# Hybrid decoder block on one core: adaLN row sums by products with a column of ones, part of them inside the second norm, the gate in the last columns' weights, last rows in halves, another order

## The chip, the cores and the metric

The kernel runs on one core of a Trainium2 chip. The metric is device time in microseconds (us) of one execution; lower is better. A kernel's time is the median of its runs. The profile is one further execution; its span runs from the first to the last instruction.

PE is the matmul engine and PEld its weight load, DVE the vector engine, ACT the scalar engine, POOL the general engine, SP the one whose queue issues most DMAs.

## The reference

One decoder block over 256 tokens of width 2048, in f32. A vector `c` gives, through one large product, six rows: shift, scale and gate for the two halves of the block.

```python
mod = silu(c) @ w_ada + b_ada                    # 2048 x 12288
sh1, sc1, g1, sh2, sc2, g2 = split(mod, 6)
h = rms_norm(x, norm1_g) * (1 + sc1) + sh1
q, k, v, gb, gc, xt = split(h @ w_in, 6)         # 2048 x 6144
attn = causal_attention(rms_norm(q), rms_norm(k), v)   # 8 heads of 128
conv = gb * causal_dwconv(gc * xt, conv_w, conv_b)
x = x + g1 * (concat(rms_norm(attn), rms_norm(conv)) @ w_out)
h2 = rms_norm(x, norm2_g) * (1 + sc2) + sh2
u_gate, u_up = split(causal_dwconv(h2 @ w_ffn_up), 2)  # 2048 x 11264
x = x + g2 * ((silu(u_gate) * u_up) @ w_ffn_down)      # 5632 x 2048
```

With 256 tokens the attention has a single block, so it is plain causal attention.

## The kernel before

Weights stream from HBM once, in 512 KB pieces (`raw`, 128 x 1024). Every weight and activation is split into a high part and a low part, `hi` on ACT (L938) and `lo = raw - hi` on DVE or POOL (L949), and each matmul of f32 precision is made of three in a faster format: high by high, high by low, low by high (L1185 to L1187). In the up projection the two products with the high weights are one matmul of 512 columns (L1536), and the third has 256 (L1540).

The work is a list of **slots**: the input projection (its twelve column groups of 512, named q0 to x1, in the order of `CFG['turns']`), the output projection (A and C parts), then the up projection z and the down projection D in four segments. A slot is up to four weight blocks and their matmuls. Function `slot(i)` writes out, in this order: the split of the weights of slot i + 2 (`split_hi`, `split_lo`), the small tasks that fall due, and the matmuls of slot i. `CFG['hi_late']` lists the slots whose split comes after the early tasks instead of ahead of them. The engines run what is written in that order; `CFG['move']`, `after`, `mid`, `pre`, `carry` shift tasks by slots or positions, and how many accumulation steps stand between them. Nothing else decides the order: an instruction waits only for its operands and buffers.

**adaLN** (class `Ada`). Parts 0 to 5 are the six rows of 2048 values; SH1 = 0, SC1 = 1, G1 = 2, SH2 = 3, SC2 = 4, G2 = 5. Each part is made in column groups. Some accumulate on PE (`crep` as weights, L1025, four row groups of the array at once, tiles `ada`), the others on DVE, a step for every 128 rows of the matrix (L1042). Either way the result is 128 x n, and the row of values is the sum over its 128 partitions. For shift and scale it is needed as a column, 128 channels on 128 partitions: `cols` transposes every chunk of 128 columns by PE (L1080, bank `adac`), DVE sums along the free axis (L1082, `adaz`), and `finish` writes A (scale) or B (shift). `evac` brings the accumulators of PE to SBUF (`adae`). For the gates, `spread` and `broadcast` make rows `gB` of 128 equal partitions.

**The start** is a hand-written order, `CFG['start']`: `sc` and `sh` are the scale and shift products of the first two chunks (their halves 0 and 1, then `e` for evacuation and `c` for the columns), `tr` and `out` transpose x and copy it out (`xn`, `xnT`), `p n b` splits block b of slot n, `h` makes the modulated input, `go n h` issues matmuls of slot n. It also sets the order in which the first loads are issued on SP's queue.

**The second norm** (`norm2`, L1397 on): squares on ACT, a root by DVE and ACT, a diagonal `n2d` by DVE, a product `n2b` on PE that spreads it, then `h2_chunks` for the first eight chunks of the up projection's input. PE has one load of adaLN ahead of `n2b` and a part of it behind.

**The end.** Columns are worked in pairs of groups of 512, f = 0, 1 and then 2, 3, both token halves t in each. `gate_down` folds the gate and the residual into x1 for the first segments. In the last segment `evac_down` multiplies the bank by the gate row (L1504), adds x1 (L1505) and stores 128 x 512 (L1506); the last slots belong to f = 2 and f = 3.

**Sums and seeds.** A column group whose partial sum leaves PSUM is added by DVE when it comes back (L1207), or, where `CFG['seed']` names it, copied back into PSUM by ACT first (L1194) and copied out by ACT again (L1205).

## Time and profile before

| | us |
|---|---|
| median of 3 runs | 1174.42 (1174.08 to 1176.89) |
| the profiled execution | 1174.33 |
| its span | 1172.2 |
| DMA moved | 320.21 MB, mean 273 GB/s |
| 42 to 100 us: PE busy of 58.0 | 58.0 |
| 165 to 427 us: PE busy of 262.0 | 262.0 |
| 435 to 1139 us: PE busy of 704.0 | 704.0 |

A row of the profile's groups names the line, the engine, the operation, what it writes and reads, the shape and the count, then busy time, mean duration in ns, idle time of the engine before it and what ended that. In the timeline a row has its start and length. PE's matmuls overlap, and their ends are modelled: how long one takes in a stream is read from the distance of starts, not from a row's length. An f32 product shows as two records, a transpose and a matmul of the split format as one.

### The profile page before, as it was taken

How to read it: one execution, taken by the hardware profiler on the slowest of the kernel's cores; microseconds unless marked ns; L12 is line 12 of the kernel's file. 1: busy time of each engine (PE TensorE's matmuls, PEld its weight loads, DVE VectorE, ACT ScalarE, POOL GpSimd, SP SyncE). 2: the span in 40 equal slices, each digit the busy share in tenths (PEclk: the TensorE clock that was granted, in tenths of full speed). 3: DMA queues.
4: the chain of work that ended last, by engine and by line, in shares of the span. 5: the costliest groups of instructions: out<-in, count | busy, mean ns of one | idle time of the engine just before them, and what ended most of it. 6: DMA issues, size and time to landing. Idle time of an engine off the chain costs nothing.

```text
span 1172.2 us, 17007 instructions
## 1 busy us (share of the span) xinstructions
PE 1148.8 (98%) x5945; PEld 960.4 (82%) x5945; DVE 928.4 (79%) x1318; ACT 635.9 (54%) x981; POOL 169.4 (14%) x103
## 2 busy tenths in 40 slices
PE   4999999999999999999999999999999999999998
PEld 2778788888777878888888888888888888888886
DVE  4669989997888989999999544768887897666785
ACT  4664455469665445546676445555435554445461
POOL 0668684530001111000000000000000000000000
PEclk9999999999999999999999999999999999999999
DMA  9999999995799989986565755576887877875541
GB/s 350 404 406 364 387 381 373 397 389 171 228 395 319 344 292 358 377 276 208 159 208 186 235 179 179 174 234 216 284 296 272 301 243 229 284 256 175 171 153 72
DMA packets 205381, 320.21 MB, mean 273 GB/s; under 512 B 13816, under 2 KB 112300, under 8 KB 205296
## 3 DMA queue, kind: packets, MB, share of 16 engines
q1 hardware_dynamic: 202336, 314.68, 77.2%
q10 hardware_dynamic: 2352, 4.22, 1.3%
q8 instruction: 46, 0.75, 0.3%
q14 instruction: 39, 0.32, 0.1%
q0 software_dynamic: 608, 0.23, 0.1%
HBM read 314.87 MB, written 4.21 MB: 272 GB/s over the span
## 4 chain that ended last, share of the span: by engine, by line
PE 91%; DVE 5%; DMA 2%; ACT 1%; issue 1%; SPq 0%; ACTq 0%; DVEq 0%
PE z L1536 27%; PE z L1540 14%; DVE ada L1042 2%; PE ada L1025 1%; PE mv L1185 1%; PE mv L1187 1%; PE mc L1185 1%; PE mv L1186 1%; PE mc L1187 1%; PE mc L1186 1%; PE mx L1185 1%; PE mx L1187 1%; PE mx L1186 1%; PE mg L1185 1%; PE mg L1187 1%; PE mg L1186 1%
## 5 line engine op out<-in xcount | busy, mean ns | idle before, releaser
L938 ACT ACTIVATE hi<-raw 128x1024 fp32r<-128x1024 f32 (+1 forms) x401 | 401.1, 1030 | 324.7 <-PE z L1536 100.9
L949 DVE TENSOR_TENSOR lo<-raw,hi 128x1024 fp32r<-128x1024 f32 x342 | 399.0, 1204 | 99.8 <-ACT hi L938 94.3
L1536 PE MATMUL z<-h,hi 128*128 128x512 f32 x1408 | 328.6, 390 | 0.0
L1536 PEld LDWEIGHTS z<-h,hi 128*128 128x128 f32 x1408 | 261.4, 188 | 52.7 <-DVE h L1431 0.3
L1042 DVE SCALAR_TENSOR_TENSOR ada<-raw,csil,ada 128x512 f32<-128x512 f32 (+2 forms) x215 | 188.9, 891 | 3.6
L949 POOL TENSOR_TENSOR lo<-raw,hi 128x1024 fp32r<-128x1024 f32 x59 | 147.0, 2511 | 274.3 <-ACT hi L938 231.6
L1540 PEld LDWEIGHTS z<-h,lo 128*128 128x128 f32 x1408 | 174.8, 192 | 3.4
L1540 PE MATMUL z<-h,lo 128*128 128x256 f32 x1408 | 176.0, 283 | 0.0
L1101 POOL MEMSET gb<- 128x512 f32 x2 | 1.0, 524 | 491.9 <-DVE uy L1475 491.9
L1452 DVE TENSOR_TENSOR ub<-z,ub 128x256 f32<-128x256 f32 x120 | 43.7, 416 | 34.9 <-ACT ub L1449 34.7
L1449 ACT ACTIVATE ub<-z 128x256 f32<-128x256 f32 x120 | 39.4, 382 | 30.9 <-PE z L1536 30.8
L1468 ACT ACTIVATE uy<-ub,vcols 128x256 f32<-128x256 f32 x88 | 45.6, 594 | 6.8 <-DMA gr<-gs 6.7
L1473 DVE SCALAR_TENSOR_TENSOR uy<-ub,vcols,uy 128x255 f32<-128x255 f32 x88 | 42.1, 478 | 5.7 <-ACT uy L1468 5.6
L1475 DVE SCALAR_TENSOR_TENSOR uy<-ub,vcols,uy 128x254 f32<-128x254 f32 x88 | 42.5, 483 | 3.1
L1484 ACT ACTIVATE gh<-uy 128x512 fp32r<-128x512 f32 x22 | 13.8, 629 | 38.8 <-DVE uy L1482 38.8
L1478 ACT ACTIVATE uy<-uy 128x512 f32<-128x512 f32 x22 | 13.9, 633 | 37.9 <-DVE uy L1475 37.9
L1185 PE MATMUL mq<-hi,h 128*128 128x512 f32 x64 | 25.8, 403 | 3.8 <-DVE xnT L2026 2.8
L1485 DVE TENSOR_TENSOR gl<-uy,gh 128x512 fp32r<-128x512 f32 x22 | 15.2, 692 | 18.0 <-ACT gh L1484 18.0
L1025 PE MATMUL ada<-raw,crep 128*32 128x512 f32 (+1 forms) x224 | 26.2, 565 | 2.6 <-DVE rst L882 1.9
L1185 PE MATMUL mc<-hi,h 128*128 128x512 f32 x64 | 25.5, 398 | 0.5 <-ACT pa_q L1205 0.5
L1185 PE MATMUL mg<-hi,h 128*128 128x512 f32 x64 | 25.7, 402 | 0.0
L1185 PE MATMUL mv<-hi,h 128*128 128x512 f32 x64 | 25.3, 395 | 0.2 <-DVE pa_g L1207 0.2
(570 smaller groups left out, 1913.7 us busy)
## 6 DMA issues: line engine op xcount, KB each, us to landing
raw<-in_w_ada_dram SPq DMA_DIRECT2D x180, 512.0 KB, 6.5
raw<-in_w_ffn_up_dram SPq DMA_DIRECT2D x352, 256.0 KB, 4.5
raw<-in_w_in_dram SPq DMA_DIRECT2D x95, 512.0 KB, 7.3
raw<-in_w_ffn_down_dram SPq DMA_DIRECT2D x76, 512.0 KB, 4.3
raw<-in_w_out_dram SPq DMA_DIRECT2D x32, 512.0 KB, 5.4
raw<-in_w_ada_dram SPq DMA_DIRECT2D x24, 256.0 KB, 6.3
raw<-in_w_ffn_down_dram SPq DMA_DIRECT2D x24, 256.0 KB, 3.8
xr<-in_x_dram SPq DMA_DIRECT2D x4, 512.0 KB, 6.0
```

The costliest lines, as they stand in the source:

```text
L938: act(piece(his, "hi")[:, :m], t[:, :m], AF.Copy)
L949: (nc.gpsimd if pool in (i + 1, 3) else V).tensor_tensor(out=piece(los, "lo")[:, :m], in0=t[:, :m], in1=hi[:, :m].bitcast(F32), op=ALU.sub ...
L1042: V.scalar_tensor_tensor(out=self.acc[n], in0=v, scalar=csil[:, i:i + 1], in1=acc, op0=ALU.mult, op1=ALU.add)
L1185: mm(o, a, hi[k], start=(first and k == 0 and not seeded), stop=False, skip_group_check=True)
L1186: mm(o, a, lo[k], start=False, stop=False, skip_group_check=True)
L1187: mm(o, b, hi[k], start=False, stop=(last and k == nk - 1), skip_group_check=True)
L1452: V.tensor_tensor(out=d, in0=zp[grp][ft][:, :256], in1=d, op=ALU.add)
L1468: act(y, b, AF.Identity, bias=fcols[3][:, i:i + 1], scale=fcols[2][:, i:i + 1])
L1473: V.scalar_tensor_tensor(out=y[:, 1:], in0=b[:, :255], scalar=fcols[1][:, i:i + 1], in1=y[:, 1:], op0=ALU.mult, op1=ALU.add)
L1475: V.scalar_tensor_tensor(out=y[:, 2:], in0=b[:, :254], scalar=fcols[0][:, i:i + 1], in1=y[:, 2:], op0=ALU.mult, op1=ALU.add)
L1536: mm(zp[grp][ft], blk(hi, j)[:, ft * P:(ft + 1) * P], h2T[k + j], start=k + j == ks[0], stop=k + j == ks[1] - 1)
L1540: mm(zp[grp][ft][:, :256], blk(lo, j)[:, ft * P:(ft + 1) * P], h2T[k + j][:, :256], start=False, stop=False)
```

## The change

Five edits are made together.

1. `cols` no longer transposes. Each chunk of 128 columns is the weights of one f32 product with a column of ones, so that PE sums over partitions; `finish` reads PSUM, and the reductions on DVE are gone.
2. `CFG['gap']` names two column groups, part 4 from chunk 0 (eight chunks) and part 3 from chunk 4 (four). Their `cols` is issued inside `norm2`, between `n2d` and `n2b`.
3. For the last segment's f = 3, `split_hi` multiplies the raw weights by the gate row ahead of the split, in eight DVE multiplies of 128 x 512; the evacuation of those columns then only adds x1.
4. The last slot's second token half runs as two column halves of 256, and its evacuation and store are in halves too.
5. The tables change: the order of the start, which adaLN groups have load buffers of their own (`own`, 256 KB pieces), spans of their loads, seeds (c0 1, q0 1 and v1 2 come in, c1 3 goes), `hi_late`, two turns that swap, counts of accumulation steps, and many shifts of tasks.

```diff
-CFG = {'ada': [[1, 2, 256, True, 0, 2], [0, 2, 256, False, 0, 5], [1, 4, 512, False, 2, 8], [0, 4, 512, True, 4, 5],
+CFG = {'gap': [[4, 0], [3, 4]],
+ 'ada': [[1, 2, 256, True, 0, 1], [0, 2, 256, False, 0, 3], [1, 4, 512, False, 2, 8], [0, 4, 512, True, 4, 5],
...
- 'seed': ['c0 3', 'c1 3', 'k1 2', 'k1 3', 'x0 1'],
+ 'seed': ['c0 1', 'c0 3', 'k1 2', 'k1 3', 'q0 1', 'v1 2', 'x0 1'],
...
- 'own': [[0, 2], [0, 0], [1, 2]],
+ 'own': [[1, 2], [0, 4], [1, 4], [0, 2]],
...
-    def split_hi(nb):
+    def split_hi(nb, gate=None):
...
             t = take()
+            for a in range(0, m, 512) if gate else ():
+                V.tensor_tensor(out=t[:, a:a + 512], in0=t[:, a:a + 512], in1=gB[gate], op=ALU.mult)
             act(piece(his, "hi")[:, :m], t[:, :m], AF.Copy)
...
                 p = bank(f"adac{self.part}_{self.c0}", full=False)
-                if self.nch == 1:
-                    mm(p[:, 0:1], self.chunk(0), ones[:, 0:1], start=True, stop=True)
-                    z = p[:, 0:1]
-                else:
-                    for k in range(m):
-                        nc.tensor.transpose(p[:, k * P:(k + 1) * P], self.chunk(a + k), ident)
-                    z = bank(f"adaz{self.part}_{self.c0}")[:, :m]
-                    V.tensor_reduce(out=z, in_=p[:, :m * P].rearrange("p (k q) -> p k q", q=P), axis=AX.X, op=ALU.add)
-                self.finish(z, self.c0 + a, m, scale)
+                for k in range(m):
+                    mm(p[:, k:k + 1], self.chunk(a + k), ones[:, 0:1], start=True, stop=True)
+                self.finish(p[:, :m], self.c0 + a, m, scale)
...
-    def mm_tok(key, hi, lo, kts, nk, first, last, by_t=False):
+    def mm_tok(key, hi, lo, kts, nk, first, last, by_t=False, in_halves=False):
...
+            if in_halves and t == 1:
+                break
...
+        for c in (slice(0, 256), slice(256, 512)) if in_halves else ():
+            for k in range(nk):
+                a, b = (v[:, P:] for v in kts[k])
+                mm(o[:, c], a, hi[k][:, c], start=False, stop=False, skip_group_check=True)
+                mm(o[:, c], a, lo[k][:, c], start=False, stop=False, skip_group_check=True)
+                mm(o[:, c], b, hi[k][:, c], start=False, stop=k == nk - 1, skip_group_check=True)
...
             V.tensor_scalar(d[:, t * P:(t + 1) * P], ident, r[:, t:t + 1], None, op0=ALU.mult)
+        for g in gap:
+            g.cols()
         p = bank("n2b", full=False)
...
-                V.tensor_tensor(out=y, in0=p, in1=gB[G2, f], op=ALU.mult)
-                V.tensor_tensor(out=y, in0=y, in1=x1[t, f], op=ALU.add)
-                nc.sync.dma_start(out[0, t * P:(t + 1) * P, f * 512:(f + 1) * 512], y)
+                w = 256 if (f, t) == (3, 1) else 512
+                for a in range(0, 512, w):
+                    c = slice(a, a + w)
+                    if f < 3:
+                        V.tensor_tensor(out=y[:, c], in0=p[:, c], in1=gB[G2, f][:, c], op=ALU.mult)
+                    V.tensor_tensor(out=y[:, c], in0=y[:, c] if f < 3 else p[:, c], in1=x1[t, f][:, c], op=ALU.add)
+                    nc.sync.dma_start(out[0, t * P:(t + 1) * P, f * 512 + a:f * 512 + a + w], y[:, c])
...
-        at(s + 2, g.cols)
+        if [g.part, g.c0] in CFG["gap"]:
+            gap.append(g)
+        else:
+            at(s + 2, g.cols)
```

On PE at the start of the program, before: the second half of the shift products (`ada_0_0` from the small load buffers), the transposes of x (`xn`), the transposes for the columns (`adac`) and the first main matmul (`mq`).

```order
L1025 MATMUL ada_0_0_251<-raw_133,crep 32x256 x2
L2020 MATMUL xn_270<-ident,xr 128x128 x4
L1080 MATMUL adac_0_279<-ident,adae_0_275 128x128 x2
L2020 MATMUL xn_285<-ident,xr 128x128 x4
L1080 MATMUL adac_0_290<-ident,adae_0_277 128x128 x2
L2020 MATMUL xn_297<-ident,xr 128x128 x4
L2020 MATMUL xn_302<-ident,xr 128x128 x4
L2020 MATMUL xn_311<-ident,xr 128x128 x4
L1185 MATMUL mq_342<-hi,h_331 128x512
```

The same place on PE in the changed kernel; `pv_vbc` is the transpose of the bias vectors.

```order
L1027 MATMUL ada_0_0_205<-raw,crep 32x256 x8
L2034 MATMUL xn_244<-ident,xr 128x128 x4
L869 MATMUL pv_vbc<-ident,vb 128x112
L2034 MATMUL xn_255<-ident,xr 128x128 x4
L2034 MATMUL xn_262<-ident,xr 128x128 x4
L2034 MATMUL xn_269<-ident,xr 128x128 x4
L1027 MATMUL ada_0_0_205<-raw,crep 32x256 x8
L1078 MATMUL adac_0_310<-ones,adae_0_304 128x1 x2
L1078 MATMUL adac_0_323<-ones,adae_0_315 128x1 x2
L1183 MATMUL mq_337<-hi,h_333 128x512
```

Four transposes of x moved from behind the shift products to between their halves, the bias vectors' transpose came there too, and the sums now stand directly ahead of the first main matmul.

On PE at the second norm, before: the last transposes of x1 (`x1t`), adaLN's products (`ada_8`) and `n2b`.

```order
L1353 MATMUL x1t_4281<-ident,x_11_3824 128x128
L1025 MATMUL ada_8_0_4297<-raw,crep 32x512 x12
L1405 MATMUL n2b<-n2d,ones 128x256
L1025 MATMUL ada_8_0_4297<-raw,crep 32x512 x4
L1353 MATMUL x1t_4415<-ident,x_02_3818 128x128
```

The same place in the changed kernel.

```order
L1357 MATMUL x1t_4263<-ident,x_11_3824 128x128
L1027 MATMUL ada_8_0_4279<-raw,crep 32x512 x12
L1078 MATMUL adac_0_4321<-ones,ada_0_3119 128x1 x4
L1078 MATMUL adac_0_4328<-ones,ada_0_3119 128x1 x4
L1078 MATMUL adac_4_4335<-ones,adae_4_3628 128x1 x4
L1411 MATMUL n2b<-n2d,ones 128x256
L1027 MATMUL ada_8_0_4279<-raw,crep 32x512 x4
```

Twelve sums, each two records on the chip, came in ahead of `n2b`; their transposes stood some slots earlier.

On DVE at the end of the program, before: the last splits of weights, then four evacuations of a multiply and an add each.

```order
L949 TENSOR_TENSOR lo<-raw,hi 128x1024 x2
L1504 TENSOR_TENSOR d_11345<-m('D', 3, 2)0_11221,gB_2_9735 128x512
L1505 TENSOR_TENSOR d_11345<-d_11345,x_02_10057 128x512
L1504 TENSOR_TENSOR d_11349<-m('D', 3, 2)1_11222,gB_2_9735 128x512
L1505 TENSOR_TENSOR d_11349<-d_11349,x_12_10059 128x512
L1504 TENSOR_TENSOR d_11353<-m('D', 3, 3)0_11257,gB_2_9735 128x512
L1505 TENSOR_TENSOR d_11353<-d_11353,x_03_10093 128x512
L1504 TENSOR_TENSOR d_11357<-m('D', 3, 3)1_11258,gB_2_9735 128x512
L1505 TENSOR_TENSOR d_11357<-d_11357,x_13_10095 128x512
```

The same place in the changed kernel.

```order
L951 TENSOR_TENSOR lo<-raw,hi 128x1024
L939 TENSOR_TENSOR raw<-raw,gB_2_9729 128x512 x2
L951 TENSOR_TENSOR lo<-raw,hi 128x1024
L1514 TENSOR_TENSOR d_11353<-m('D', 3, 2)0_11218,gB_2_9729 128x512
L1515 TENSOR_TENSOR d_11353<-d_11353,x_02_10051 128x512
L1514 TENSOR_TENSOR d_11357<-m('D', 3, 2)1_11219,gB_2_9729 128x512
L1515 TENSOR_TENSOR d_11357<-d_11357,x_12_10053 128x512
L1515 TENSOR_TENSOR d_11361<-m('D', 3, 3)0_11257,x_03_10087 128x512
L1515 TENSOR_TENSOR d_11364<-m('D', 3, 3)1_11258,x_13_10089 128x256 x2
```

The multiplies of f = 3 moved from the evacuations to the raw weights, and the last add is in two halves.

## The prediction

> **What bounds the kernel now.** I read the page first: the engines' busy time, the slices, and the chain that ended last.

> ```profile
> PE 1148.8 (98%) x5945; PEld 960.4 (82%) x5945; DVE 928.4 (79%) x1318; ACT 635.9 (54%) x981; POOL 169.4 (14%) x103
> PE   4999999999999999999999999999999999999998
> PE 91%; DVE 5%; DMA 2%; ACT 1%; issue 1%; SPq 0%; ACTq 0%; DVEq 0%
> ```

> PE is busy in all slices but the first and last, and 91% of the chain is PE. So the time is the sum of PE's work, and only what lies on PE, or makes PE wait, counts. I then asked for PE's waits (engine, line, what ended them, us in total, times, longest) and for four stages (stretch, its length, then busy us and instructions of PE, PEld, DVE, ACT and POOL, granted clock, DMA share, GB/s).

> ```profile
> PE n2b L1405 <- DVE n2d L1403: 1.2, 1, 1.2
> PE mq L1185 <- DVE adaz L1082: 1.0, 1, 1.0
> ...
> PE adac L1080 <- DVE adae L1042: 0.5, 1, 0.5
> PE mc L1185 <- ACT pa_q L1205: 0.5, 1, 0.5
> PE mv L1185 <- DVE pa_g L1207: 0.2, 1, 0.2
> ```

> ```profile
> 0.00:28.00 28.00, 12.90 (x98) 6.71 (x98) 10.63 (x29) 12.93 (x25) 1.60 (x9) 1.00 0.96 349
> ...
> 100.00:165.00 65.00, 63.34 (x289) 51.79 (x288) 61.68 (x90) 25.87 (x29) 45.34 (x22) 1.00 1.01 373
> ...
> 1139.00:1163.00 24.00, 24.00 (x108) 19.87 (x107) 13.05 (x17) 7.21 (x8) 0.00 (x0) 1.00 0.16 61
> 1163.00:1172.20 9.20, 4.59 (x21) 3.46 (x19) 5.36 (x8) 0.00 (x0) 0.00 (x0) 0.97 0.29 114
> ```

> What an order can win is small. Once the main products run, PE waits 1.2 in the second norm and 1.0 + 0.5 + 0.5 + 0.2 = 2.2 us elsewhere; the rest is the first 28 us and the last 5.

> **Row sums by products.** Sixty-four column chunks of adaLN (four parts of 16) were transposed, one PE record each, and a reduction on DVE summed the rows. Each becomes one f32 product whose weights are the chunk and whose moving operand is one column of ones. The kernel has four such products already, for the sums of squares ssA and ssC (here from the timeline and the chain; start, length).

> ```profile
> 88.10 0.87 PE adac L1080 x8
> 337.79 0.61 PE L1798 MATMUL ssA<-ones,sq 128*128 128x1 f32 x4
> 338.26 0.52 PE L1843 MATMUL trc<-ident,pa_c 128*128 128x128 f32 x3
> 370.57 0.50 PE L1798 MATMUL ssC<-ones,sq 128*128 128x1 f32 x4
> 370.93 0.49 PE L1185 MATMUL m('C', 0)0_3690<-hi,mix 128*128 128x512 f32 x1
> L1798 PEld LDWEIGHTS ssA<-ones,sq x4: 186/190/192, 337.8 to 338.1; 128*128 128x128 f32 x4
> ```

> A transpose costs 0.87 / 8 = 0.109 us. The ssA sums are two products in the code, but four records and four weight loads; the next instruction starts at 338.26, 0.47 us later, so 0.235 each. For ssC it is 370.93 - 370.57 = 0.36, or 0.18 each. Four records in 0.47 are 0.12 us apart though each moves one column: the load of the 128x128 weights sets the pace, and it is paid twice. I take 0.223 a chunk, nearest to four records at a steady pace with the last one partly hidden, and 0.18 and 0.235 as its ends. So a chunk costs PE 0.114 us **more** than before (0.07 to 0.126).

> [...]

> Four chunks lie in the first 28 us, where PE mostly idles, and count in the start below; twelve go into the second norm. The other 48 stand among matmuls that never pause: 48 x 0.114 = **+5.5 us** (+3.4 to +6.0).

> What leaves DVE:

> ```profile
> L1082 DVE TENSOR_REDUCE adaz<-adac x18: 432/690/700, 23.5 to 521.0; 128x4 f32<-128x512 f32 x14, 128x2 f32<-128x256 f32 x4
> L1207 DVE TENSOR_TENSOR pa_q<-mq,pa_q x10: 674/682/692, 122.1 to 208.0; 128x512 f32<-128x512 f32 x10
> ```

> Eighteen reductions of 0.43 to 0.69 go, 14 x 0.69 + 4 x 0.43 = 11.4 us, and six adds of 0.68 (three more groups are seeded through ACT, which gains 12 copies and has room: 25.87 busy of 65 in the stage from 100 to 165). DVE is not PE, so this is worth only the waits that it ends. In that stage DVE is busy 61.68 of 65 us, so it sheds what PE waited for there.

> **Waits in the body.** I count two as gone: mq behind adaz (1.0), whose reduction goes, and mc behind pa_q (0.5), since the split of slot 4 now comes after that evacuation (hi_late gains 2). The adae and pa_g waits (0.7) stand behind accumulations that all remain; I leave them. **-1.5 us** (0 if new ones take their place, -2.2 if all go).

> **Sums inside the second norm.** Parts 4, columns 0 to 7, and 3, columns 4 to 7, move to where PE waits 1.24 us for n2d. Twelve chunks take 12 x 0.223 = 2.7 us there, 1.4 more than the wait holds, so n2b comes that much later; but 12 x 0.109 = 1.3 us of transposes vanish from PE ahead of it. Behind n2d, five small DVE instructions (0.16 each) must end before the first h2f; they run while PE is still in the sums. Net **+0.1 us** (-1.3 if the sums fitted into the wait, +0.3 with the dearer product).

> **Gate and last rows.** Eight DVE multiplies of the last columns' weights, 128x512, like the one at 1168.35 below, add 8 x 0.69 = 5.5 us; DVE is busy 13.05 of 24 us in the stage from 1139 to 1163, which hides them. Without that cover they would cost up to 5.5. In the tail:

> ```profile
> 1167.62 0.69 DVE L1504 TENSOR_TENSOR d<-m('D', 3, 3)1_11258,gB 128x512 f32<-128x512 f32 x1
> 1168.35 0.69 DVE L1505 TENSOR_TENSOR d<-d,x 128x512 f32<-128x512 f32 x1
> L1452 DVE TENSOR_TENSOR ub<-z,ub 128x256 f32<-128x256 f32 x120 | 43.7, 416 | 34.9 <-ACT ub L1449 34.7
> 442.80 7.28 PE z L1536 x32
> 450.08 3.83 PE z L1540 x32
> DMA to landing us min/median/max: 2.2/2.3/2.3
> ```

> After the last matmul DVE now does 0.69 + 0.04 + 0.69 = 1.42 us; then it does one add of 256 columns from PSUM, 0.42. Six matmuls of 512 columns (7.28 / 32 = 0.2275) become twelve of 256 (3.83 / 32 = 0.12): +0.08. The last store has half the bytes; its landing takes 2.3 us for 256 KB, between 0 and half of which may go: I take 0.2. Together **-1.1 us** (-0.9 to -2.1).

> **The start.** Issues of SP, then PE and DVE around the first main product, from the timeline:

> ```profile
> 4.45 12.32 SPq L998 DMA_DIRECT2D raw<-in_w_ada_dram  x12
> ...
> 17.44 1.97 PE L2020 MATMUL xn<-ident,xr 128*128 128x128 f32 x8
> 19.34 3.18 PE L1025 MATMUL ada<-raw,crep 128*32 128x256 f32 x32
> ...
> 23.93 1.47 PE L2020 MATMUL xn<-ident,xr 128*128 128x128 f32 x12
> 28.25 0.77 PE L1185 MATMUL mq<-hi,h 128*128 128x512 f32 x1 [2.84 <-DVE xnT L2026]
> 28.81 0.63 PE L1186 MATMUL mq<-lo,h 128*128 128x512 f32 x1
> 29.24 0.63 PE L1187 MATMUL mq<-hi,h 128*128 128x512 f32 x1
> ...
> 25.01 0.69 DVE L2026 COPY xnT<-xn 128x512 f32<-128x512 f32 x1
> 25.62 1.89 DVE L2041 TENSOR_TENSOR lo<-raw,hi 128x512 fp32r<-128x512 f32 x3
> 27.42 0.68 DVE L2026 COPY xnT<-xn 128x512 f32<-128x512 f32 x1
> 28.02 0.40 DVE L1617 TENSOR_SCALAR hf<-xnT,A,B 128x256 f32<-128x256 f32 x1
> 28.53 0.42 DVE L1622 TENSOR_TENSOR h<-hf,h 128x256 fp32r<-128x256 f32 x1
> ```

> The main products begin at 28.25, 5.7 us after the last shift matmul (19.34 + 3.18 = 22.5). Against the change: one more load of w_in, 512 KB, now stands among the twelve of adaLN and ahead of the shift's; at 349 GB/s it puts them back by 1.5 us. Between the shift's halves PE now does four transposes of x, 16 records; 12 took 1.47 us, so 2.0 us, largely under that later load. For it: between the shift and the first product DVE loses two reductions (0.43 each), two copies to xnT (0.69 + 0.68) and one of three splits (1.89 / 3 = 0.63), and gains one pair hf and h (0.40 + 0.42), as h of row block 1 now comes first: 0.86 + 1.37 + 0.63 - 0.82 = 2.0 us. Late by 1.5 to 2.0 and shorter by 2.0: I call that even. Six of eight transposes of x now precede the first product instead of seven, so 4 x 0.109 = 0.4 falls behind it. **+0.4 us** (-0.9 if the load is hidden, +3.5 by rival two).

> **Sum.** The profiled execution took 1174.33 us (span 1172.2 and 2.1 around it), beside the median of 1174.42. To it come 5.5 - 1.5 + 0.1 - 1.1 + 0.4 = +3.4: **1177.7 us**.

> **Rivals.**
> One: the products are cheap, since PE loads their weights behind the 512-wide matmuls ahead of them. For it speaks that ssC, behind such a matmul, took 0.36 where ssA took 0.47: one load of four, 0.11, was hidden. Against it: only one. If both loads of a chunk were hidden, 0.235 - 2 x 0.11 = 0.015 us would be left: 48 x (0.015 - 0.109) = -4.5, the norm -1.3, the rest as above with all waits gone: -4.5 - 1.3 - 2.2 - 1.1 + 0.4 = -8.7, **1165.6 us**. [...]

> Two, slower: the start slips. The place is the shift's second half on PE. If the 16 transpose records ahead of it run as the eight at 17.44 did (1.97, 0.25 each), they take 3.9 us instead of 2.0, and the first main product comes 1.9 us later. The first ones ran at 0.43 apart (28.81, 29.24) against 0.2275 for the same shape later; after a longer wait six more could, 6 x 0.2 = 1.2. 3.4 + 1.9 + 1.2 = +6.5, **1180.8 us**. For it speaks that PE starts these stages slowly in this trace; against it that the twelve at 23.93 were fast. It decides from a first main product after 29 us. [...]

> Three: the order gains all it can. All 2.2 us of waits go and the first product is 1.3 us earlier: 5.5 - 2.2 + 0.1 - 1.1 - 0.9 = +1.4, **1175.7 us**.

> **How the numbers follow.** Forecast 0.50, rival one 0.13, two 0.20, three 0.17. A measurement of this kernel can tell about 0.3%, 3.5 us, from no change: 1170.9 to 1177.9. Rival one is faster; rival three and 0.30 of the forecast lie within; 0.20 of the forecast and rival two are slower: 0.13, 0.47, 0.40. All terms at their low ends give 3.4 - 2.2 - 1.3 - 2.1 - 0.9 = -3.1, 1171.2 us; all at the high ends 6.0 + 0 + 0.3 - 0.9 + 3.5 = +8.9, 1183.2 us. That all fall on one side is unlikely, so the range is 1171.5 to 1182; rival one stays outside.

> **What would show it.** In the profile after: each adac product as two records some 0.11 us apart, near 14 us for all (step one), or half of that (rival one); no wait of mq for an adac reader; PE's wait ahead of n2b gone and n2b over 1 us later against its neighbours; the last matmul to the end 3.2 us instead of 4.6; the first mq near 28.2. The prediction is wrong if the products run faster than the transposes did, or if PE shows waits over 2 us in all that were not there.

## The result, and the profile after

The changed kernel takes **1191.59 us** (median of 4 runs, 1190.00 to 1192.84) beside 1174.45 (median of 4 runs) for the kernel before: 17.1 us more, a ratio of 1.0137 (95% interval 1.0124 to 1.0149). The prediction was 1177.7, in a range to 1182. Its profiled execution has a span of 1190.2 us.

From the page of the changed kernel, the engines' busy time, PE's slices and the shares of the chain that ended last:

```profile
PE 1161.7 (98%) x6015; PEld 971.1 (82%) x6015; DVE 923.9 (78%) x1301; ACT 641.4 (54%) x993; POOL 170.5 (14%) x103
PE   4989999999999999999999999999999999999998
PE 88%; DVE 5%; DMA 4%; issue 2%; ACT 1%; SPq 0%; DVEq 0%; ACTq 0%
```

PE is busy 12.9 us longer for 70 records more, and PE's share of the chain fell from 91 to 88%, with 4% of DMA in its place. The third slice is no longer full. PE's waits (engine, line, what ended them, us in total, times, longest), without those of the first 28 us:

```profile
PE mg L1183 <- ACT pa_v L1209: 3.3, 1, 3.3
PE at L1731 <- DVE adae L1044: 1.9, 1, 1.9
...
PE mc L1183 <- ACT pa_q L1209: 1.6, 2, 1.3
PE mv L1183 <- DVE pa_k L1211: 1.4, 1, 1.4
PE mg L1183 <- ACT pa_k L1209: 0.8, 1, 0.8
```

Of the waits of before, those for n2d and for adaz are gone; that of mc for pa_q grew from 0.5 to 1.6, and the list as shown comes to 9.0 us, of which 7.1 lie between 41 and 100 us. The stages there, of before and then of after (stretch, length, busy us and instructions of PE, PEld, DVE, ACT, POOL, granted clock, DMA share, GB/s):

```profile
60.00:80.00 20.00, 20.00 (x97) 13.75 (x96) 13.24 (x17) 12.82 (x19) 12.87 (x16) 1.00 1.04 406
```

```profile
60.00:80.00 20.00, 15.99 (x64) 10.39 (x63) 5.48 (x5) 9.17 (x15) 4.52 (x4) 0.83 1.04 410
80.00:100.00 20.00, 18.63 (x95) 14.72 (x94) 14.06 (x18) 13.89 (x20) 18.95 (x17) 1.00 0.73 237
```

The DMA engines deliver as much as before from 60 to 80 us, and all four compute engines do less with it; the clock is 0.83. The transfers only fall back behind that (237 GB/s). So a slower DMA is not what starved PE. The place shows in four rows on PE and SP (the issue of the loads) and in ACT's timeline:

```profile
56.92 0.39 PE L1185 MATMUL mk<-hi,h 128*128 128x512 f32 x1
64.09 1.06 PE L1027 MATMUL ada<-raw,crep 128*32 128x512 f32 x8
65.91 0.50 PE L1183 MATMUL mg<-hi,h 128*128 128x512 f32 x1 [0.75 <-ACT pa_k L1209]
```

```profile
52.37 2.30 SPq L1000 DMA_DIRECT2D raw<-in_w_ada_dram  x4
```

```profile
58.45 1.58 ACT L1209 ACTIVATE pa_x<-mx 128x512 f32<-128x512 f32 x3 [0.19 <-DMA raw<-in_w_ada_dram]
65.25 1.09 ACT L1209 ACTIVATE pa_k<-mk 128x512 f32<-128x512 f32 x2 [5.23 <-PE ada L1027]
66.23 2.01 ACT L940 ACTIVATE hi<-raw 128x1024 fp32r<-128x1024 f32 x2
71.52 0.60 ACT L1209 ACTIVATE pa_v<-mv 128x512 f32<-128x512 f32 x1 [3.28 <-DVE ada L1044]
```

The last product of mk ends at 57.3 us, but ACT copies it out at 65.25, after 5.2 us idle. By its semaphores the copy waits for one of the four half loads of adaLN issued from 52.37 us on, landed at 59.96, and for PE's products that read them, at 64.09, behind all of mv. It reads neither. The link is the tile: pa_k, pa_v and the half loads `raw2` take theirs from one ring, t2k, of 41. (The section on the change calls them load buffers of their own; they are not.) With four groups in 'own' 48 half loads go through it, where before had 24, and pa_k's turn now falls on tiles of loads that have only just been issued. Everything queued behind the copy on ACT stands still, so DVE and POOL lack `hi`, pa_v comes late in the same way, and PE waits 3.3 us for that.

### The profile page after: what moved, and what is told of

Same layout as the page of the kernel before. It is cut to its first block, busy times and chain, and to the rows that moved or that the text cites. A ratio compares the mean times of both kernels' runs of the same rounds, so it can differ in the third digit from the quotient of the medians.

```text
span 1190.2 us, 17190 instructions
## 1 busy us (share of the span) xinstructions
PE 1161.7 (98%) x6015; PEld 971.1 (82%) x6015; DVE 923.9 (78%) x1301; ACT 641.4 (54%) x993; POOL 170.5 (14%) x103
## 4 chain that ended last, share of the span: by engine, by line
PE 88%; DVE 5%; DMA 4%; issue 2%; ACT 1%; SPq 0%; DVEq 0%; ACTq 0%
PE z L1546 27%; PE z L1550 14%; DVE ada L1044 3%; DMA raw<-in_w_ada_dram 2%; PE ada L1027 1%; DMA raw<-in_w_in_dram 1%; PE mx L1183 1%; PE mx L1184 1%; PE mx L1185 1%; PE mg L1183 1%; PE adac L1078 1%; PE mg L1185 1%; PE mg L1184 1%; PE mq L1183 1%; PE mq L1185 1%
## 5 line engine op out<-in xcount | busy, mean ns | idle before, releaser
L951 DVE TENSOR_TENSOR lo<-raw,hi 128x1024 fp32r<-128x1024 f32 x342 | 404.0, 1219 | 118.0 <-ACT hi L940 114.3
```

Source lines behind the costliest of these rows:

```text
L951: (nc.gpsimd if pool in (i + 1, 3) else V).tensor_tensor(out=piece(los, "lo")[:, :m], in0=t[:, :m], in1=hi[:, :m].bitcast(F32), op=ALU.sub ...
```

## The experiments

**First: order or code, and which part of the code.** e1_code is the changed code with the tables of before; e2_order the other way round.

```diff
 # e1_code: after
-CFG = {... of after}
+CFG = {... of before, 'gap': [[4, 0], [3, 4]]}
 # e2_order: before
-CFG = {... of before}
+CFG = {... of after}
```

> The four edits of the code (row sums by products, sums inside the second norm, gate in the weights, last rows in halves) under the tables of before. Theory A, the tables cost most: 1174.4 + 5.5 + 0.1 - 1.1 = 1179, and no wait of PE over 2 us between 60 and 100 us, where after has one of 3.3 and a clock of 0.50. Theory B, the products cost it all, by what waits for them: near 1191. The products on PE: two records each, 0.22 us a chunk.

> The tables of after (order, loads, seeds) with the code of before: sums by transposes and reductions, no sums inside the norm, gate and rows as before. Theory A: 1191.6 - 4.5 = 1187, with the wait of PE near 69 to 72 us and the half clock behind it as in after. Theory B: within 2 us of before, 1174 to 1176, with neither.

e1_code took 1183.76 us (ratio 1.0071, 1.0054 to 1.0088), e2_order 1183.93 (1.0080, 1.0056 to 1.0104), beside 1174.80. Each half costs 9 us, and 18 together are about the whole. Neither theory of one cause holds: with the old code the tables were to cost 12 us or none, and the code under the old tables 5 or 17. PE's waits, between 424 and 460 us in e1_code and between 40 and 100 us in e2_order:

```profile
PE z L1547 <- ACT adae L1063: 3.6, 1, 3.6
```

```profile
PE mg L1185 <- ACT pa_v L1205: 3.2, 1, 3.2
PE mv L1185 <- DVE pa_k L1207: 1.8, 1, 1.8
PE mc L1185 <- ACT pa_q L1205: 1.6, 2, 1.1
...
PE mg L1185 <- ACT pa_k L1205: 0.8, 1, 0.8
```

The waits of 41 to 100 us belong to the tables: they are there with the old code and absent in e1_code. The code has a wait of its own behind the second norm; it stands only under the old tables, not in after, so that the two halves add up to the whole so closely is luck. The half clock that was expected in e2_order did not come: behind the same wait the granted clock of its profiled execution stays at 1.00, as it does from 40 to 1170 us.

Two parts of the code alone: e3_transposes is after with the transposes and reductions back, e4_tail is before with the gate in the weights and the last rows in halves.

```diff
 # e3_transposes: after
-                for k in range(m):
-                    mm(p[:, k:k + 1], self.chunk(a + k), ones[:, 0:1], start=True, stop=True)
-                self.finish(p[:, :m], self.c0 + a, m, scale)
+                ...
+                    for k in range(m):
+                        nc.tensor.transpose(p[:, k * P:(k + 1) * P], self.chunk(a + k), ident)
+                    z = bank(f"adaz{self.part}_{self.c0}")[:, :m]
+                    V.tensor_reduce(out=z, in_=p[:, :m * P].rearrange("p (k q) -> p k q", q=P), axis=AX.X, op=ALU.add)
+                self.finish(z, self.c0 + a, m, scale)
```

> After, with only the row sums put back to transposes and reductions. If a product costs PE 0.114 us more than a transpose: 1191.6 - 5.5 - 1.3 (twelve chunks in the norm) = 1185 to 1186. If the products cost more by what waits for them (theory B): below 1180. If DVE needs the time that its reductions take again: 1187 to 1190.

> Before, with only the gate folded into the last columns' weights and the last rows in halves. 1174.4 - 1.1 = 1173.3; 3.2 us from the last matmul to the end, where before has 4.6. If the eight multiplies on DVE are not hidden: 1174 to 1178.

e3_transposes: 1184.96, 6.6 us below after and at the 1185 that was expected. That is luck in part: the expectation had no term for the half clock behind runs of products, found below, which went too, nor for waits that are new in this run (1.4 us for h behind the norm, 1.0 for pa_c). e4_tail: 1174.79 beside 1174.80 (ratio 0.9997, 0.9984 to 1.0010), no difference that can be measured; from the last product to the end it takes 4.19 us, where 3.2 were expected.

**Second: the ring, the clock, and the norm.** In after the granted clock was 0.50 in three places beside the start. One, 71 to 78 us, follows the wait of 3.3 us. At the others PE waits for nothing. The second norm, PE's timeline and its clock (stretch, length, PE busy, granted clock, DMA share, GB/s):

```profile
443.44 1.95 PE L1078 MATMUL adac<-ones,ada 128*128 128x1 f32 x16
445.25 1.03 PE L1078 MATMUL adac<-ones,adae 128*128 128x1 f32 x8
446.14 0.68 PE L1411 MATMUL n2b<-n2d,ones 128*128 128x256 f32 x2
446.75 1.90 PE L1027 MATMUL ada<-raw,crep 128*32 128x512 f32 x8
448.58 1.89 PE L1357 MATMUL x1t<-ident,x 128*128 128x128 f32 x8
```

```profile
446.00:447.00 1.00, 1.00 (x9) 0.93 1.01 364
447.00:448.00 1.00, 1.00 (x8) 0.50 0.98 340
...
450.00:451.00 1.00, 1.00 (x6) 0.87 1.05 352
```

Twelve chunks run in 2.70 us (0.225 each, where the prediction had 0.223), and behind them 3.4 us at half clock. The same stands behind the other run of twelve (529.86 to 532.7 us). I suspected that the clock takes products of one column for idle time. e6_wide gives each product 64 moving columns, of which the first is read; e5_own takes two groups out of the ring.

```diff
 # e5_own: after
- 'own': [[1, 2], [0, 4], [1, 4], [0, 2]],
+ 'own': [[1, 2], [0, 2]],
 # e6_wide: after
-                    mm(p[:, k:k + 1], self.chunk(a + k), ones[:, 0:1], start=True, stop=True)
-                self.finish(p[:, :m], self.c0 + a, m, scale)
+                    mm(p[:, 64 * k:64 * k + 64], self.chunk(a + k), ones[:, 0:64], start=True, stop=True)
+                self.finish(p[:, 0:64 * m:64], self.c0 + a, m, scale)
 # e7_probe: before, with blocks that nothing reads
+    def probe(n, w):
+        p = bank("probe", full=False)
+        for j in range(n):
+            mm(p[:, :w], (ident, ones, c32)[j % 3], ones[:, :w], start=True, stop=True)
+    ...
 # e8_nogap: e1_code
-       'gap': [[4, 0], [3, 4]]
+       'gap': []
```

> After, with only two of its four groups of adaLN columns loaded in halves into the ring of 2 KB tiles (parts 0 and 1 from column 2; the two from column 4 go into the ring of raw tiles). Theory, the ring: the evacuations pa_k and pa_v wait since their tiles are those of loads that have only just come. Then the waits of PE on pa_k and pa_v (0.8 and 3.3 us) and the half clock of 71 to 78 us go: 1191.6 - 4.1 - 3.4 = 1184, or 1186 if some of it comes back later. Rival, the loads come too late by their order: waits of 3 us stay between 55 and 90 us, and the time is within 2 us of 1191.6.

> After, with 64 moving columns of ones in place of one in each row sum (the result is read from the first of them). Theory, the clock: long stretches of one-column products count as idle, so they end in 3.3 us at half clock behind the norm and behind the twelve products at 530 us, where PE waits for nothing. Wider products take the same 0.22 us a chunk, since the loads of the weights set it, and keep the clock: 1191.6 - 1.7 - 1.7 = 1188. Rival, the clock falls for another reason: half clock at both places as before, 1191.6. If the columns count: 24 us of products in place of 14, 1196 or more.

> Before, with blocks of products more in the FFN that nothing reads: 4, 8, 12, 12, 12, 16, 24 and 48 of one moving column, 12, 24 and 48 of 64, 24 of 128, and 12 of one again. Each product is two records 0.11 us apart with 1 and with 64 columns, so 0.22 us. Theory, the clock: behind the blocks of 24 and 48 with one column the granted clock is 0.50 for 3.3 us at least, behind those of 12 (2.7 us) sometimes, behind 4 and 8 never; behind those of 64 and 128 columns never. Rival: 1.00 throughout.

> The edits of the code under the tables of before, without the sums inside the second norm: those two groups of columns are summed in their own slots again. In the run with them PE waited 3.65 us for adae behind the norm and had half the clock for 6.5 us, 3.2 lost; the 1.24 us for n2d come back. If the norm is the cause: 1183.8 - 3.65 - 3.2 + 1.2 = 1178. If the products cost this wherever they stand: 1182 to 1185.

e5_own took 1182.21 us, 9.4 below after. The same stage of it, and ACT's copies of mk:

```profile
60.00:80.00 20.00, 20.00 (x98) 13.76 (x97) 11.77 (x14) 12.48 (x19) 14.98 (x17) 1.00 1.04 405
```

```profile
54.78 1.28 ACT L1209 ACTIVATE pa_k<-mk 128x512 f32<-128x512 f32 x2 [0.34 <-PE mk L1185]
```

PE is full again, pa_k waits only for its own input, and no wait of PE on a pa tile is left. Moving those two groups also changes the rings that their loads wait for, but the order in which the groups are wanted is the same, which speaks against the rival (loads too late by their order). The spans of the two profiled executions are 10.6 us apart: 7.1 of waits on pa tiles and 3.4 for the 6.8 us at half clock behind the longest. Two other half clocks balance: the one near 532 us is gone, and one of 3.4 us at 256 us is new, behind a wait of 1.9.

e6_wide took 1188.04, 3.6 below after, the size that the clock theory had. Its norm:

```profile
440.67 2.00 PE L1078 MATMUL adac<-ones,ada 128*128 128x64 f32 x16
442.50 1.06 PE L1078 MATMUL adac<-ones,adae 128*128 128x64 f32 x8
443.40 0.65 PE L1411 MATMUL n2b<-n2d,ones 128*128 128x256 f32 x2
443.98 1.07 PE L1027 MATMUL ada<-raw,crep 128*32 128x512 f32 x8
444.97 1.09 PE L1357 MATMUL x1t<-ident,x 128*128 128x128 f32 x8
```

The products take the same 0.227 us each with 64 times the columns, and the eight records behind them 1.07 and 1.09 us instead of 1.90 and 1.89. This run alone does not show that the width is the reason, for it also moved the products against the windows of the clock (3.413 us, worked out from e15_probe2 below), of which none holds more than 1.77 us of either run; e7_probe and e12_own_wide show it.

e7_probe (1258.6 us with its added work) shows both by themselves. Four blocks of it: 12 products of 64 columns from 931.4 us, 24 from 967.5, 24 of 128 from 1006.2 and 48 of 64 from 1098.6; then the last of three blocks of 12 with one column, from 824.0 to 826.6:

```profile
932.00:936.00 4.00, 4.00 (x36) 1.00 0.34 101
967.00:974.00 7.00, 7.00 (x64) 1.00 1.00 359
1006.00:1013.00 7.00, 7.00 (x64) 1.00 0.58 186
1098.00:1111.00 13.00, 13.00 (x108) 1.00 0.60 202
824.00:827.00 3.00, 3.00 (x29) 0.99 0.36 115
827.00:830.00 3.00, 3.00 (x16) 0.50 0.76 242
```

With 64 or 128 columns the clock never fell, in up to 10.6 us of nothing else. With one column it fell behind all blocks of 12 and more (for some blocks of 12 I had expected it not to), not behind those of 4 and 8.

e8_nogap took 1179.94 us (ratio 1.0032), 3.8 below e1_code, where 5.8 was expected: the sums inside the norm are what e1_code paid for there.

**Third: do the remedies add up, and can the cheap forms gain?** e12_own_wide is after with both edits. e9_order, e10_gap and e11_tail use transposes, and write the add of the last rows' first half ahead of the second half's products. e9_order has the tables of e5_own, e10_gap those of before with the twelve sums inside the norm, e11_tail those of before.

```diff
 # e9, e10, e11: in mm_tok, between the two halves
                 mm(o[:, c], b, hi[k][:, c], start=False, stop=k == nk - 1, skip_group_check=True)
+            if c.start == 0:
+                early(o, c)    # the add of x1 and the store of these columns
 ...
```

> The tables of after, with two groups in the ring of 2 KB tiles as in e5_own, row sums by transposes and reductions, sums inside the norm and the gate in the weights as in after; of the last rows, the first half is added while PE still works on the second. If ring, products and their half clock are all that after lost: 1185.0 (e3_transposes) - 9.4 (as e5_own against after) - 0.7 (tail) = 1175. If the rest of the order costs too: 1178 to 1181, with waits of PE of over 1 us that before does not have.

> The tables of before, transposes and reductions, twelve of them inside the second norm, gate in the weights, last rows in halves with the first added early. Twelve transposes are 1.3 us, the wait for n2d 1.24: 1174.8 - 1.2 - 0.7 = 1173. Rival: PE waits some 3.6 us for adae behind the norm as in e1_code, and the clock halves: 1176.5 to 1179.

> Before, with the gate in the weights and the last rows in halves, the add of the first half now written ahead of the second half's products. If both adds waited for the last product because they follow it in the program: the first starts some 0.7 us ahead of it, one add of 0.42 us is left, and from the last product to the end it takes 3.6 us where e4_tail has 4.19 and before 4.61: 1174.8 - 0.6 = 1174. If PE has to wait until the first half is read: a wait of PE of 0.4 us or more in the last stage, and 1174.8 to 1175.3.

> After, with both remedies: two groups in the ring as in e5_own, and 64 moving columns in the row sums as in e6_wide. If they add up: 1191.6 - 9.4 - 3.6 = 1178.6, and no half clock between 40 and 1170 us. If the same loss was counted in both: 1181 to 1182.

e12_own_wide: 1178.46, 13.1 below after; 9.4 + 3.6 = 13.0. They add up, as far as the runs can tell: those of e5_own alone lie between 1179.39 and 1185.38, and beside the runs of before made with them, the ratios give 10.8 and 5.2 us for the two and 12.7 for both. Between 40 and 1170 us its clock is 1.00 throughout. Its clock in the slices behind the twelve products of the norm (432.37 to 435.10) and behind the other twelve (517.54 to 520.13):

```profile
435.00:436.00 1.00, 1.00 (x9) 0.51 (x12) 0.16 (x1) 0.21 (x1) 0.00 (x0) 1.00 1.01 352
520.00:521.00 1.00, 1.00 (x7) 0.87 (x7) 0.82 (x3) 0.74 (x2) 0.00 (x0) 1.00 1.09 385
```

Counted in windows of 3.413 us (e15_probe2 below) from its half clock at the start (28.78 us), 2.59 us of these products lie in one window both times, more than the 2.32 us that halved the clock near 532 us in after. So here it is the 64 columns that keep the clock. It is still slower than before (ratio 1.0029, 1.0016 to 1.0041).

e11_tail: 1177.53, slower, because of my edit. From its DVE timeline:

```profile
1166.36 0.42 DVE L1538 TENSOR_TENSOR d<-m('D', 3, 3)1_11264,x 128x256 f32<-128x256 f32 x1 [8.23 <-PE m('D', 3, 3)1_11264 L1198]
1166.70 0.68 DVE L1527 TENSOR_TENSOR d<-m('D', 3, 2)0_11224,gB 128x512 f32<-128x512 f32 x1
```

In DVE's order the early add also stands ahead of the other evacuations, and held them while DVE waited for it 8.2 us; the tail grew to 6.47 us. PE, too, waited 0.5 us until the first half was read, before it wrote the second half of the same tile. So whether an early add could gain is left open; within one tile it holds PE up. e9_order and e10_gap carry the same tail, about 2.3 us more than e4_tail's 4.19. Without it e9_order's 1178.88 would be near 1176.6, where 1175 was expected.

e10_gap: 1186.21; even less 2.3 for the tail that is 9.7 us above before. The rival's mechanism held, a wait for adae and half a clock, but at over twice its size (7.9 us where it had 3.6), and the time lies above its 1179. PE and DVE at its norm:

```profile
432.10 1.07 PE L1028 MATMUL ada<-raw,crep 128*32 128x512 f32 x8
441.03 1.97 PE L1366 MATMUL x1t<-ident,x 128*128 128x128 f32 x8 [7.86 <-ACT adae L1063]
```

```profile
431.27 0.69 DVE L1085 TENSOR_REDUCE adaz<-adac 128x4 f32<-128x512 f32 x1
432.28 0.69 DVE L1085 TENSOR_REDUCE adaz<-adac 128x4 f32<-128x512 f32 x1
433.29 0.69 DVE L1085 TENSOR_REDUCE adaz<-adac 128x4 f32<-128x512 f32 x1
```

Twelve transposes fit the wait, but their three reductions then stand on DVE ahead of h2f, and PE waits 7.9 us for a copy that ACT has behind the h it makes from h2f. What such sums cost hangs on the tables: e9_order has the same twelve transposes inside its norm, and PE waits there only 1.4 us, for h.

**Fourth: what was left.** e13_products is before with products alone, e14_order the tables of e5_own with transposes, no sums in the norm, and after's gate and last rows. e15_probe2 has blocks of 8 to 11 products.

> Before, with only the row sums made products. Sixty chunks off the start at 0.223 instead of 0.109 us are +6.8; two waits for the reductions (1.3 and 0.5 us) go: 1174.3 + 5 = 1179.3, so that products are what is left in e12_own_wide. If the rest of the order is what is left there: 1174 to 1176. If the run of twelve products near 520 us halves the clock: 1.7 more.

> The tables of after with two groups in the ring as in e5_own, transposes and reductions, no sums inside the norm, gate and last rows as in after. If products are what is left in e12_own_wide: within 1.5 us of before, 1173 to 1175.5. If the rest of the order costs: 1176 to 1179, with waits of PE over 1 us between 40 and 420 us.

> Before, with blocks in the FFN of 8, 9, 10, 11, 9, 10, 11, 8, 11, 10, 9 and 8 products of one moving column that nothing reads, and 24 of 16 columns. In e7_probe 12 (2.6 us) halved the clock 4 times in 4, and 8 (1.7 us) not. If the share of idle time in a fixed window of some 3.3 us decides, 11 and 10 do it in some places and not in others, and 8 never; if there is a fixed length, each length behaves alike. Sixteen columns: like 64, never, if a few columns are enough; else as one column.

e13_products: 1180.20 beside 1174.65 (ratio 1.0047, 1.0033 to 1.0061), **+5.5 us**. e14_order: 1176.42 (1.0014, 1.0004 to 1.0024), +1.8, which by its expectation says that the rest of the order costs too; its PE waits 2.2 us for adae near 163 us, with half the clock behind that. But that wait is no sure mark of the order: the profiled execution of e4_tail, with the tables of before, has one of 2.5 us and half a clock in the same place, where before has 0.5. So the price of the products is the larger part of what e12_own_wide still loses, and whether the order has a part in it stays open.

In e15_probe2 the clock fell for some blocks of one length and not for others (times from the timeline; the fall worked out from the share of the slice in which it happens):

```
products   block, us            half clock from
11         783.96 to 786.33     786.6
9          711.44 to 713.37     714.9
9          821.24 to 823.17     824.1
9          1028.10 to 1030.03   -
10         748.38 to 750.53     -
10         853.51 to 855.66     -
10         991.40 to 993.55     994.8
11         883.00 to 885.37     885.6
11         954.10 to 956.47     957.3
8          676.87, 918.96, 1065.49 (1.70 long)   -
```

Two of the slices that it is worked out from:

```profile
714.00:715.00 1.00, 1.00 (x10) 0.95 0.85 283
824.00:825.00 1.00, 1.00 (x8) 0.57 0.26 31
```

The falls lie 71.7, 37.5, 61.4, 71.7 and 37.5 us apart: 21, 11, 18, 21 and 11 times 3.413, a length worked out from the 279.9 us between the first and the last, 82 windows; by the slices the half clock behind each lasted 3.40 to 3.42 us. On that grid every block of 9 or more that lies in one window halved the next one, and the three that a boundary cuts (1028.9, 749.0, 854.9) did not, with at most 1.49 us in one window. (One block of 9 starts 0.06 us ahead of its window.) The blocks of 8 were all cut, as were those of 4 and 8 and the 12 of 64 columns in e7_probe, so 8 is open, and of the wide blocks only those of 24 and 48 tell. For products the limit lies near 1.9 us in these runs: 1.87 and 1.93 us halved the next window here, 1.92 us near 518 us in e8_nogap did not. The block of 24 with 16 columns, 6.5 us long, halved two windows (1114.3 to 1121.1 us): 16 columns did not keep the clock either.

Waits show the same in all these profiles, the start left out. A wait of PE halved the next window in each of the nine places where 1.78 us or more of it lay in one window (1.78 in e3_transposes, 44.15 to 45.93 us, with half the clock from 46.4), and in none of the windows at full clock where it was 1.67 us or less. (A window at half clock can be followed by another with less: 0.79 us in after, at 71.4 us.) That is why e2_order kept its clock: a boundary at 70.75 us cuts its wait of 3.25 us into 1.58 and 1.67, where in after 2.47 us of it lay in one window.

## Why the prediction was wrong

**Row sums: right, in size too.** +5.5 was predicted for 48 products; e13_products shows +5.5 for 60 of them, less the waits for reductions (the records themselves take 6.6 us longer there, 0.109 a product where 0.114 was priced). They are two records 0.11 us apart with 1, 64 and 128 columns alike (e7_probe, 0.22 us a product); that the weights' load, one to a record (e6_wide has 128 loads for its 128 records), sets that pace is the reading that is left, an estimate: no run varied the weights. Rival one (cheap products) is out.

**Waits in the body: the step that failed.** The prediction put "-1.5 us (0 if new ones take their place, -2.2 if all go)". Of its two waits the one for adaz went and the one for pa_q grew; a longer set came in, and the term had no end above 0. The prediction gave the change of 'own' no term. It doubles the half loads in a ring whose tiles the evacuations need, and what hung on it was 9.4 us: waits, and half a clock behind the longest. Waits over 2 us in all that were not there are the prediction's own sign that it is wrong. That the tables cost this is shown by e2_order and e5_own; that the tile ties pa_k to the load is read from its semaphores and the ring, and agrees with e5_own, where the wait is gone.

**What a run of products does to the clock: missing.** No term had it. Between the transposes of x1 and the first z of the norm, before takes 435.01 - 427.27 = 7.74 us, e6_wide 446.19 - 436.99 = 9.20, and after 450.20 - 439.77 = 10.43. Less the 1.31 of transposes that left the slots ahead, e6_wide is 0.15 above before: the +0.1 of the prediction, as long as the clock holds. After pays 1.2 more there, and more behind the second run of twelve; e6_wide puts both at 3.6 (two stretches of 3.4 us at half clock lose 1.7 each). The prediction had slow matmuls only behind a wait, in rival two, and only at the start; the price of half a clock behind a new wait in the body had no term either. In e3_transposes a wait with 1.78 us in one window of 3.413 us was enough to halve it. What I did not ask is what counts as busy in such a window.

**Gate and last rows: right in sign, half in size.** From the last product to the end, after takes 3.96 us where before took 4.61 and 3.2 was expected (the prediction's own terms, 1.0 for DVE and 0.2 for the store, give 3.4):

```profile
1186.24 0.76 DVE L1515 TENSOR_TENSOR d<-m('D', 3, 3)1_11258,x 128x256 f32<-128x256 f32 x2 [0.74 <-PE m('D', 3, 3)1_11258 L1191]
```

DVE sits idle for 0.74 us and then does both halves, 0.04 us behind the last product: both follow it in the program and read its tile. And from the last add to the end it is 3.2 us as before (1190.17 - 1187.0 and 1172.19 - 1169.04), so the smaller store landed no sooner. Alone the edit can't be told from no change (e4_tail).

**Start: a little better than forecast.** The first main product begins at 27.20 us, not 28.25: -1.05 against +0.4, a little past the low end of -0.9. What made it earlier was not looked into.

**The sum.** 5.5 for the products, 9.4 for the ring and 3.6 for the clock are 18.5; the start and the tail give back 1.05 + 0.65 = 1.7. That is 16.8 of the 17.1 us measured. It leaves out what the sums in the norm save (e12_own_wide, without ring and clock, is 4.2 us over before) and what the order costs beside the ring (1.8 in e14_order, gate and last rows included), which would have to balance nearly; the first was not measured alone, so the close agreement is in part luck. No version here beats the kernel before.

## What to carry to other kernels

Before loads are moved into a ring of tiles, count its takers in program order: a buffer shared by prefetches and by evacuations ties the evacuation to the prefetch, and every instruction queued behind it waits too (the copy of pa_k stood 5.2 us in after). A product of one column took PE as long here as one of 128 (0.22 us each in e7_probe), and a run of twelve cost the clock besides (0.50 for 3.4 us behind the norm in after); give them 64 columns, which took no longer here (0.227 us each in e6_wide) and kept the clock (putting wide ones between them was not tried). A busy PE in the profile isn't a PE whose clock holds (in after PE is busy 1.00 of 447 to 448 us, at a clock of 0.50): read the granted clock in slices of 1 us.
